# Dilated attention with rotary turning on 64 or on 128 partitions, a head's steps two or three blocks behind, and one sum of raw weights on POOL or on DVE

## The chip, the core and the metric

One core of a Trainium2 chip runs a block of two layers for 512 tokens of 1024 features in float32. The metric is the device time of one execution in microseconds (us), as the median of several. TensorE (PE) does the matmuls. VectorE (DVE), ScalarE (ACT) and GpSimd (POOL) work beside it, each through its own list of instructions in order, and SyncE (SP) starts the transfers of the weights. An engine that meets an instruction whose input isn't ready waits there, with all that stands behind it.

## The reference

Layer 0 mixes tokens by a gated recurrence, layer 1 by dilated attention; each is followed by a gated feed-forward part, and a vector `c` modulates norms and gates through `ada_w`. The change lies in layer 1:

```python
def apply_partial_rope(t, cos, sin):          # the first 32 of a head's 128 features
    t1, t2 = t[..., :16], t[..., 16:32]
    return concatenate([t1 * cos - t2 * sin, t2 * cos + t1 * sin, t[..., 32:]])

proj = (u @ w_in).reshape(B, S, 3, 3, 8, 128)       # group, q/k/v, head, feature
for gi, (window, dilation) in enumerate(((128, 1), (512, 4), (2048, 16))):
    q = apply_partial_rope(proj[:, :, gi, 0], cos, sin) * 128 ** -0.5
    k = apply_partial_rope(proj[:, :, gi, 1], cos, sin)
    o_g, lse_g = dilated_group_attention(q, k, proj[:, :, gi, 2], window, dilation)
wts = softmax(stack(lses))                          # weights of the three groups
o = einsum('gbsh,gbshd->bshd', wts, stack(outs))
y = o.reshape(B, S, 1024) @ w_out
```

## The kernel before

Each float32 product is made from three matmuls: weights and activations are cut into a high and a low part (`hi`, `lo`), and `three` (L427 to L430) multiplies hi by hi, lo by hi and hi by lo. ACT casts the high part of a weight tile (L84), and DVE subtracts it to get the low one (L85). `Stream` keeps two raw tiles of weights in flight and three pairs of parts. Its list `items` mixes attention weights with tiles of `ada_w`; these are reduced on DVE by one TENSOR_SCALAR (L245) and three SCALAR_TENSOR_TENSOR (L247) per tile, and then on POOL.

**Attention, 705 to 1126 us.** For each of 8 heads and 3 groups, two blocks of 24 matmuls of 128x512 make q and k, one block each. `qk_evac` (L1669) copies a block from the accumulator to `qk` (L1675) and its first 32 rows once more to a tile `turning` (L1676): q's rows on partitions 0 to 31, k's on 32 to 63, 512 tokens in columns. After k, `turn_pair` (L1680) turns both at once on DVE, by a shuffle of rows, two multiplications with the tables `cs` and an addition (L1683 to L1686), and ACT copies the results back into `qk` (L1689). For group 0 the copies and evacuations reorder the tokens, so they write strided.

A counter in `fl` (`Fillers`) ticks once per block. From the tick n at which a head starts, its steps are hung on later ticks: the scores of its three groups (L1710 for group 0, L1728 for groups 1 and 2) at n+2, n+4 and n+6, the merging weights at n+8, the transposes of the probabilities (`flips_r`, `flips_n`; matmuls L1777, their copies L1782 on ACT and L1784 on DVE) at n+9 and n+10, and the products with the values (`pv_r` L1804, `pv_n` L1813 and L1815) at n+10 and n+11. Steps of the last head, for which no blocks are left, go into `tail`, among the matmuls of the output projection.

**Values.** The values of groups 1 and 2 come from `seven_values`, which stands in the list of work after head 0's group 1 and again after head 4. A unit (one group, 512 features) takes two raw tiles of weights and makes four quarters of the product out of seven products of sums, each 24 matmuls of 128x256. `prepare` makes the operands: `cut` is a cast on ACT (L1371) and a subtraction on DVE (L1372). In its step 1, three sums on DVE (L1390 to L1392) follow a first sum on POOL (L1389); the casts of the later pieces use their results. The products are combined into V on DVE (L1426 to L1440).

The order of the instructions in each engine's list isn't the order of the code: a scheduler that estimates times orders them ahead of compilation. Time depends on which waits PE meets in that list.

Of the kernel before, what the change touches and what calls it, by code (L numbers as in the profile page):

```python
# [9 lines left out]
F32 = mybir.dt.float32  # L10
F32R = mybir.dt.float32r
I32 = mybir.dt.int32
AF = mybir.ActivationFunctionType
OP = mybir.AluOpType

P = 128
S = 512
# [18 lines left out]
class Stream:  # L36
# [31 lines left out]

    def fill(self):
        real = lambda i: self.items[i][1] is not None  # L70
        while self.loaded < len(self.items) and sum(map(real, range(self.done, self.loaded))) + real(self.loaded) <= self.raws:
            self._load(self.loaded)
            self.loaded += 1
# [78 lines left out]
def block_kernel(tc, x, c, positions, ada_w, ada_b, norm_g, hgrn_w_in, lower, hgrn_norm_g, hgrn_w_out,  # L152
# [8 lines left out]
    with ExitStack() as ctx:  # L161
# [38 lines left out]
        shared = base.tile([P, 4, S], F32, name="shared")  # L200
        cs = shared[:, 0:2]

# [209 lines left out]
        st = Stream(nc, wp, items, 2, 3)  # L412
# [300 lines left out]
        def rotary(pl):  # L713
# [10 lines left out]
            act.dma_start(invf, inv_freq)  # L724
            a0 = pl.tile([P, S], F32, name="a0")
            a1 = pl.tile([P, S], F32, name="a1")
            dve.tensor_copy(V4(a0), L4(pos_i))
            dve.tensor_scalar(a0, a0, invf, None, op0=OP.mult)
# [630 lines left out]
        def seven_values(dsts, apart, th, tl):  # L1359
# [17 lines left out]
            def prepare(i, step):  # L1377
                if i >= len(dsts):
                    return
                if step == 0:  # L1380
                    raws[i] = [st.whole(), st.whole()]
                    place(i, 0)
                    cut(i, 0, 0, 0, 0)
                    cut(i, 0, 1, 1, 1)
                elif step == 1:
                    place(i, 1)
                    cut(i, 1, 0, 1, 0)
                    a, b = raws[i]
                    pool.tensor_add(C(b, 1), C(b, 1), C(a, 1))  # L1389
                    dve.tensor_add(C(a, 1), C(a, 1), C(a, 0))  # L1390
                    dve.tensor_add(C(a, 0), C(a, 0), C(b, 1))
                    dve.tensor_add(C(b, 0), C(b, 0), C(a, 0))  # L1392
                    cut(i, 1, 1, 0, 0)
                elif step == 2:
                    place(i, 2)
                    cut(i, 2, 1, 0, 1)
                    cut(i, 2, 0, 1, 1)
                else:
                    place(i, 3)
                    cut(i, 3, 0, 1, 0)  # L1400
                    raws.pop(i)
                    st.fill()
# [235 lines left out]
        PNs, PR_h = [h[:, k].rearrange("p (t n) -> p t n", t=4) for k in range(2)], h[:, 2].rearrange("p (t n) -> p t n", t=4)  # L1638
        flip_no = [0]
        ap = cx.enter_context(tc.tile_pool(name="a_core", bufs=1))  # L1640
# [28 lines left out]
        def qk_evac(ps, g, k, pair):  # L1669

            tl = fresh(mk, [P, S], "qk", 6)
            scale = SCALE if k == 0 else 1.0
            if k == 0:
                pair.append(fresh(mk, [64, S], "turning", 1))
            act.activation(*((tl.rearrange("p (l r) -> p l r", r=4), R4(ps)) if g == 0 else (tl, ps)), AF.Copy, scale=scale)  # L1675
            act.activation(pair[0][k * 32:k * 32 + 32], ps[0:32], AF.Copy, scale=scale)  # L1676
            pair.append(tl)
            return tl

        def turn_pair(g, pair):  # L1680
            both = pair[0]
            rot = fresh(mk, [64, S], "rot", 1)
            dve.stream_shuffle(rot, both, [(i + 16) % 32 for i in range(32)])  # L1683
            dve.tensor_mul(rot, rot, cs[0:64, 1])
            dve.tensor_mul(both, both, cs[0:64, 0])
            dve.tensor_add(both, both, rot)  # L1686
            for k in range(2):
                dst, src = pair[1 + k][0:32], both[k * 32:k * 32 + 32]
                act.copy(*((dst.rearrange("p (l r) -> p l r", r=4), R4(src)) if g == 0 else (dst, src)))  # L1689

# [128 lines left out]
        for kind, g, i in order:  # L1819
            if kind == "v":  # L1820
                if g == 1:
                    seven_values(V[1:], apart, th, tl)
                    if i:
                        act.dma_start(V[0], v_away)
                continue
            if g == 0:
                heads[i] = {}
                n = fl.n
                fl.add(n + 2, lambda i=i: scores(i, 0))
                fl.add(n + 4, lambda i=i: scores(i, 1))  # L1830
                fl.add(n + 6, lambda i=i: scores(i, 2))
                fl.add(n + 8, lambda i=i: (merge_r(i), merge_n(i)))
                fl.add(n + 9, lambda i=i: flips_r(i))
                fl.add(n + 10, lambda i=i: pv_r(i))
                fl.add(n + 10, lambda i=i: flips_n(i))
                fl.add(n + 11, lambda i=i: pv_n(i))
            whi, wlo = st.take()
            pair = []
            for k in range(2):
# [6 lines left out]
        upx.close()  # L1846
        tail = {-1: [lambda: scores(7, 2), mkx.close], 2: [lambda: merge_r(7), back(0)], 3: [lambda: merge_n(7)],
                4: [lambda: flips_r(7)], 5: [lambda: pv_r(7), lambda: flips_n(7), back(2)], 6: [lambda: pv_n(7), back(1)],
# [34 lines left out]
```

## Time and profile before

| | us |
|---|---|
| Median of 3 runs (lowest, highest) | 1529.37 (1527.95, 1531.38) |
| The profiled execution's own time | 1529.39 |
| Its span, first to last instruction | 1527.7 |
| PE busy in it | 1502.0 |
| Stretch of the attention's blocks | 705 to 1126 |
| PE busy there, of 421.0 | 409.7 |
| DVE, ACT, POOL busy there | 292.5, 215.6, 53.1 |

Busy shares are averages over stages. Where an engine sat idle, the rows in order of time give in brackets the idle time just ahead of an instruction and what ended it. PE's clock can be granted at half for a time, and the rows of stretches show the mean of the granted clock, with 1.00 for the whole.

### The profile page before, as it was taken

The numbers are of one execution on the slowest core, as the hardware profiler recorded it, in microseconds if no ns is written. First come the engines' busy times: TensorE is split into PE (matmuls) and PEld (weight loads), VectorE is DVE, ScalarE is ACT, GpSimd is POOL, SyncE is SP. The second block draws the span as 40 slices with busy tenths as digits, with TensorE's granted clock in tenths as the row PEclk, the third lists the DMA queues.
The fourth block names the chain that finished last, engine by engine and source line by source line (L and its number), as shares of the span: only waits on it lengthen the run. The fifth ranks groups of instructions, "written<-read, shape, count | busy, mean of one in ns | idle before, by whom it ended". The sixth has DMA issues, their size and how long they took to land. (4 is left out here: it accounts for less than half of the span.)

```text
span 1527.7 us, 23466 instructions
## 1 busy us (share of the span) xinstructions
PE 1502.0 (98%) x9231; PEld 1318.2 (86%) x9231; DVE 1084.8 (71%) x1830; ACT 701.1 (46%) x1119; POOL 248.4 (16%) x212
## 2 busy tenths in 40 slices
PE   8999999999999999999998999999999999999998
PEld 6777888898999988888887888988888899999886
DVE  4587867486888896576667676677666978888633
ACT  4443433353444433384535554446555534444231
POOL 1012211131222212040101121111002222221100
PEclk9999999999999999999999999999999999999999
DMA  9554444125334356333166440265213333334531
GB/s 309 178 163 146 149 134 166 56 95 153 111 111 112 112 198 233 126 110 110 56 193 179 126 138 29 94 195 155 84 42 125 91 104 110 106 105 151 185 119 56
DMA packets 206942, 199.14 MB, mean 130 GB/s; under 512 B 6840, under 2 KB 164720, under 8 KB 206576
## 3 DMA queue, kind: packets, MB, share of 16 engines
q1 hardware_dynamic: 203856, 190.87, 40.6%
q10 hardware_dynamic: 1952, 6.65, 1.2%
q8 instruction: 72, 1.18, 0.3%
q0 software_dynamic: 1024, 0.13, 0.2%
q14 instruction: 38, 0.31, 0.1%
HBM read 192.31 MB, written 5.31 MB: 129 GB/s over the span
## 5 line engine op out<-in xcount | busy, mean ns | idle before, releaser
L85 DVE TENSOR_TENSOR lo<-raw,hi 128x2048 fp32r<-128x2048 f32 x68 | 163.5, 2406 | 90.7 <-ACT hi L84 90.5
L84 ACT CAST hi<-raw 128x2048 fp32r<-128x2048 f32 x68 | 129.9, 1910 | 195.1 <-DMA raw<-in_ffn_w_out_dram 55.8
L430 PE MATMUL ps_mm<-apart,lo 128*128 128x512 f32 x384 | 151.7, 395 | 0.0
L429 PE MATMUL ps_mm<-apart,hi 128*128 128x512 f32 x384 | 151.4, 394 | 0.0
L428 PE MATMUL ps_mm<-apart,hi 128*128 128x512 f32 x384 | 150.4, 392 | 0.0
L428 PE MATMUL ps_mm<-uh,hi 128*128 128x512 f32 (+1 forms) x400 | 146.3, 366 | 0.0
L429 PE MATMUL ps_mm<-ul,hi 128*128 128x512 f32 (+1 forms) x400 | 144.3, 361 | 1.0 <-DVE ul L528 1.0
L430 PE MATMUL ps_mm<-uh,lo 128*128 128x512 f32 (+1 forms) x400 | 144.5, 361 | 0.0
L808 ACT CAST hiq<-raw 128x1024 fp32r<-128x1024 f32 x68 | 68.3, 1050 | 65.5 <-DVE raw L796 64.5
L428 PE MATMUL ps_mm<-hi,oh 128*128 128x512 f32 x240 | 94.0, 392 | 0.0
L429 PE MATMUL ps_mm<-lo,oh 128*128 128x512 f32 x240 | 93.4, 389 | 0.0
L428 PEld LDWEIGHTS ps_mm<-uh,hi 128*128 128x128 f32 x400 | 75.5, 189 | 19.7 <-issue 8.4
L429 PEld LDWEIGHTS ps_mm<-ul,hi 128*128 128x128 f32 x400 | 75.6, 189 | 12.1 <-DVE ul L528 1.5
L430 PEld LDWEIGHTS ps_mm<-uh,lo 128*128 128x128 f32 x400 | 75.5, 189 | 11.4
L428 PEld LDWEIGHTS ps_mm<-apart,hi 128*128 128x128 f32 x384 | 72.4, 189 | 14.7
L430 PEld LDWEIGHTS ps_mm<-apart,lo 128*128 128x128 f32 x384 | 72.5, 189 | 14.3
L429 PEld LDWEIGHTS ps_mm<-apart,hi 128*128 128x128 f32 x384 | 72.3, 188 | 14.4
L247 DVE SCALAR_TENSOR_TENSOR shared<-raw,cond,shared 128x512 f32<-128x512 f32 x98 | 73.2, 747 | 11.5 <-DMA raw<-in_ada_w_dram 10.7
L812 DVE TENSOR_TENSOR loq<-raw,hiq 128x1024 fp32r<-128x1024 f32 x68 | 80.1, 1219 | 0.4 <-ACT hiq L808 0.4
L249 POOL PARTITION_ALL_REDUCE shared<-shared x14 | 48.4, 3459 | 183.3 <-DVE shared L247 176.4
L792 POOL TENSOR_TENSOR raw<-raw 128x512 f32<-128x512 f32 x34 | 54.6, 1605 | 104.2 <-DVE loq L788 47.7
L796 DVE TENSOR_TENSOR raw<-raw 128x1024 f32<-128x1024 f32 x34 | 41.7, 1225 | 39.1 <-POOL raw L792 39.1
(447 smaller groups left out, 4405.5 us busy)
## 6 DMA issues: line engine op xcount, KB each, us to landing
raw<-in_ada_w_dram SPq DMA_DIRECT2D x40, 1024.0 KB, 5.2
raw<-in_ffn_w_in_dram SPq DMA_DIRECT2D x136, 256.0 KB, 3.6
raw<-in_attn_w_in_dram SPq DMA_DIRECT2D x48, 512.0 KB, 5.2
raw<-in_ffn_w_out_dram SPq DMA_DIRECT2D x22, 1024.0 KB, 4.9
raw<-in_hgrn_w_in_dram SPq DMA_DIRECT2D x12, 1024.0 KB, 5.5
raw<-in_attn_w_in_dram SPq DMA_DIRECT2D x12, 1024.0 KB, 5.1
raw<-in_ffn_w_in_dram SPq DMA_DIRECT2D x10, 1024.0 KB, 5.1
first<-in_ada_w_dram SPq DMA_DIRECT2D x14, 512.0 KB, 7.6
```

What stands on the lines that cost most here:

```text
L84: self.nc.scalar.copy(hi, t)
L85: self.nc.vector.tensor_sub(lo, t, hi.bitcast(F32))
L247: dve.scalar_tensor_tensor(a, r[:, k], sc, a, op0=OP.mult, op1=OP.add)
L249: pool.partition_all_reduce(a, a, P, bass.bass_isa.ReduceOp.add)
L428: pe.matmul(ps, ah, bh, start=start, stop=False)
L429: pe.matmul(ps, ah, bl, start=False, stop=False)
L430: pe.matmul(ps, al, bh, start=False, stop=stop)
L792: pool.tensor_add(r[:, 2], r[:, 2], r[:, 0])
L796: dve.tensor_tensor(r[:, 0:2], r[:, 0:3:2], r[:, 1:2].broadcast_to((P, 2, 512)), op=OP.add)
L808: act.copy(hi, src)
L812: dve.tensor_sub(lo, src, hi.bitcast(F32))
```

## The change

It has four parts.

1. Turning works on 128 partitions and 256 columns: q's first half of tokens, q's second, k's first and k's second take 32 partitions each. Four ACT instructions of 256 columns fill them where two of 512 did, and stand ahead of the evacuation to `qk`. The four DVE operations have 256 columns instead of 512. Four copies of 256 columns bring the result back where there were two. The place is no longer a pool's tile with one buffer but two alternating slots in `shared`, which the smaller tables leave free. The tables are built by casts of four strips.
2. All steps of a head hang one tick later. Head 6's `pv_n` then falls behind the last block and goes into `tail`. What is due at the tick at which the values come is called ahead of them.
3. The first sum of a values' unit, L1389, moves from POOL to DVE.
4. `prepare` asks the stream for one more raw tile between the two cuts of its step 2.

Where the change moves instructions is decided by the scheduler. SP's list has the same transfers in the same order before and after, and POOL's is shorter by the four sums. In PE's list, head 0's first scores stand behind 20 matmuls of the first values' product before, and behind 10 after. The values' product `pv_n` of head 0 stands where all matmuls ahead of it take 2.95 us longer than before, at 227 ns for one of 512 columns, and the scores of head 1's group 2, next behind it, where they take 3.6 us longer.

DVE's list at the second values' unit; before, from the subtractions of its two raw tiles (6605 and 6684) on. L1372 is the subtraction of a `cut`, L1390 and L1391 are sums of raw tiles, the rows with V combine products:

```order
L1372 TENSOR_TENSOR loq_6742<-raw_6605,hiq_6741 128x1024
L1372 TENSOR_TENSOR loq_6742<-raw_6684,hiq_6741 128x1024
L1433 SCALAR_TENSOR_TENSOR V_6091<-V_6091,ps_mm_6772 128x2x256
L1372 TENSOR_TENSOR loq_6802<-raw_6684,hiq_6801 128x1024
L1434 TENSOR_TENSOR V_6091<-V_6091,ps_mm_6747 128x2x256
L1435 TENSOR_TENSOR V_6091<-V_6091,ps_mm_6747 128x2x256
L1440 TENSOR_TENSOR V_6091<-V_6091,ps_mm_6811 128x2x256
L1390 TENSOR_TENSOR raw_6605<-raw_6605 128x4x256
L1436 TENSOR_TENSOR V_6091<-V_6091,ps_a_6655 128x2x256
L1372 TENSOR_TENSOR loq_6838<-raw_6684,hiq_6837 128x1024
L1391 TENSOR_TENSOR raw_6605<-raw_6605,raw_6684 128x4x256
```

The same place after (raw tiles 6614 and 6636; lines are those of the changed kernel, where L1378 is the subtraction and L1395 to L1397 are the sums):

```order
L1378 TENSOR_TENSOR loq_6751<-raw_6636,hiq_6750 128x1024
L1440 SCALAR_TENSOR_TENSOR V_6094<-V_6094,ps_mm_6781 128x2x256
L1395 TENSOR_TENSOR raw_6636<-raw_6636,raw_6614 128x4x256
L1441 TENSOR_TENSOR V_6094<-V_6094,ps_mm_6756 128x2x256
L1442 TENSOR_TENSOR V_6094<-V_6094,ps_mm_6756 128x2x256
L1378 TENSOR_TENSOR loq_6811<-raw_6636,hiq_6810 128x1024
L1396 TENSOR_TENSOR raw_6614<-raw_6614 128x4x256
L1447 TENSOR_TENSOR V_6094<-V_6094,ps_mm_6820 128x2x256
L1443 TENSOR_TENSOR V_6094<-V_6094,ps_a_6666 128x2x256
L1378 TENSOR_TENSOR loq_6847<-raw_6636,hiq_6846 128x1024
L1397 TENSOR_TENSOR raw_6614<-raw_6614,raw_6636 128x4x256
```

The sum L1395 is new in DVE's list. From the subtraction of the second raw tile to the last sum shown stand ten operations before and eleven now.

ACT's list at head 1's group 0. Before, L84 is the cast of a weight tile, and L1689 copies the turned rows of q (7174) and k (7223):

```order
L1676 ACTIVATE turning_7175<-ps_mm_7149 32x512
L1675 ACTIVATE qk_7223<-ps_mm_7198 128x512
L1676 ACTIVATE turning_7175<-ps_mm_7198 32x512
L84 CAST hi_7240<-raw_7146 128x2048
L1689 COPY qk_7174<-turning_7175 32x512
L1689 COPY qk_7223<-turning_7175 32x512
L1675 ACTIVATE qk_7272<-ps_mm_7247 128x512
```

After (q is 7186, k is 7215, L87 is the cast of the same weight tile, raw 7158, L1702 the strided copy):

```order
L1686 ACTIVATE shared<-ps_mm_7190 32x256 x2
L1687 ACTIVATE qk_7215<-ps_mm_7190 128x512
L1702 COPY qk_7186<-shared 32x2x128 x2
L1702 COPY qk_7215<-shared 32x2x128 x2
L1754 ACTIVATE h,sR_7136<-h,nR_7137 128x256 x4
L87 CAST hi_7255<-raw_7158 128x2048
```

The copies went from behind the cast to ahead of it.

DVE's list at the turning of head 1's group 2, before. L245 and L247 reduce a tile of `ada_w`, and L1784 copies head 0's transposed probabilities for `pv_n`:

```order
L1683 STREAM_SHUFFLE rot_7469<-turning_7405 64x512
L245 TENSOR_SCALAR shared<-raw_7496,cond 128x512
L1784 COPY h<-ps_a_7418 128x384
L1684 TENSOR_TENSOR rot_7469<-rot_7469,shared 64x512
L1685 TENSOR_TENSOR turning_7405<-turning_7405,shared 64x512
L247 SCALAR_TENSOR_TENSOR shared<-raw_7496,cond,shared 128x512
L1686 TENSOR_TENSOR turning_7405<-turning_7405,rot_7469 64x512
L247 SCALAR_TENSOR_TENSOR shared<-raw_7496,cond,shared 128x512 x2
```

After:

```order
L1694 STREAM_SHUFFLE rot_7455<-shared 128x256
L1695 TENSOR_TENSOR rot_7455<-rot_7455,shared 128x256
L1696 TENSOR_TENSOR shared<-shared 128x256
L88 TENSOR_TENSOR lo_7511<-raw_7500,hi_7510 128x2048
L1697 TENSOR_TENSOR shared<-shared,rot_7455 128x256
L248 TENSOR_SCALAR shared<-raw_7508,cond 128x512
L250 SCALAR_TENSOR_TENSOR shared<-raw_7508,cond,shared 128x512 x3
L1799 COPY h<-ps_a_7474 128x384
```

The whole turning now stands ahead of the modulation, and the copy behind all four of its operations.

The diff, cut to what is named here:

```diff
-    def fill(self):
+    def fill(self, most=99):
         real = lambda i: self.items[i][1] is not None
         while self.loaded < len(self.items) and sum(map(real, range(self.done, self.loaded))) + real(self.loaded) <= self.raws:
+            if most == 0:
+                return
+            most -= 1
...
-        cs = shared[:, 0:2]
+        cs = shared[:, 0].rearrange("p (a n) -> p a n", a=2)
...
-            a0 = pl.tile([P, S], F32, name="a0")
-            a1 = pl.tile([P, S], F32, name="a1")
-            dve.tensor_copy(V4(a0), L4(pos_i))
+            a0 = pl.tile([P, 256], F32, name="a0")
+            a1 = pl.tile([P, 256], F32, name="a1")
+
+            for k in range(4):
+                j, r = slice(32 * k, 32 * k + 32), 2 * (k % 2)
+                dve.tensor_copy(a0[j].rearrange("p (r l) -> p r l", r=2), L4(pos_i)[j, r:r + 2])
...
-                    pool.tensor_add(C(b, 1), C(b, 1), C(a, 1))
+                    dve.tensor_add(C(b, 1), C(b, 1), C(a, 1))
...
                     cut(i, 2, 1, 0, 1)
+                    st.fill(1)
                     cut(i, 2, 0, 1, 1)
...
             if k == 0:
-                pair.append(fresh(mk, [64, S], "turning", 1))
+                flip_no[1] += 1
+                o = flip_no[1] % 2 * 256
+                pair.append(shared[:, 1, o:o + 256])
+            for hf in range(2):
+                o = k * 64 + hf * 32
+                act.activation(pair[0][o:o + 32], ps[0:32, hf * 256:hf * 256 + 256], AF.Copy, scale=scale)
             act.activation(*((tl.rearrange("p (l r) -> p l r", r=4), R4(ps)) if g == 0 else (tl, ps)), AF.Copy, scale=scale)
-            act.activation(pair[0][k * 32:k * 32 + 32], ps[0:32], AF.Copy, scale=scale)
...
-            rot = fresh(mk, [64, S], "rot", 1)
+            rot = fresh(mk, [P, 256], "rot", 1)
             dve.stream_shuffle(rot, both, [(i + 16) % 32 for i in range(32)])
-            dve.tensor_mul(rot, rot, cs[0:64, 1])
-            dve.tensor_mul(both, both, cs[0:64, 0])
+            dve.tensor_mul(rot, rot, cs[:, 1])
+            dve.tensor_mul(both, both, cs[:, 0])
             dve.tensor_add(both, both, rot)
             for k in range(2):
-                dst, src = pair[1 + k][0:32], both[k * 32:k * 32 + 32]
-                act.copy(*((dst.rearrange("p (l r) -> p l r", r=4), R4(src)) if g == 0 else (dst, src)))
+                for hf in range(2):
+                    dst, src = pair[1 + k][0:32], both[k * 64 + hf * 32:k * 64 + hf * 32 + 32]
+                    if g == 0:
+                        act.copy(L4(dst)[:, 2 * hf:2 * hf + 2], src.rearrange("p (r l) -> p r l", r=2))
+                    else:
+                        act.copy(dst[:, hf * 256:hf * 256 + 256], src)
...
                 if g == 1:
+
+                    for fn in fl.at.pop(fl.n, []):
+                        fn()
                     seven_values(V[1:], apart, th, tl)
...
-                fl.add(n + 2, lambda i=i: scores(i, 0))
-                fl.add(n + 4, lambda i=i: scores(i, 1))
-                fl.add(n + 6, lambda i=i: scores(i, 2))
-                fl.add(n + 8, lambda i=i: (merge_r(i), merge_n(i)))
-                fl.add(n + 9, lambda i=i: flips_r(i))
-                fl.add(n + 10, lambda i=i: pv_r(i))
-                fl.add(n + 10, lambda i=i: flips_n(i))
-                fl.add(n + 11, lambda i=i: pv_n(i))
+                fl.add(n + 3, lambda i=i: scores(i, 0))
+                fl.add(n + 5, lambda i=i: scores(i, 1))
+                fl.add(n + 7, lambda i=i: scores(i, 2))
+                fl.add(n + 9, lambda i=i: (merge_r(i), merge_n(i)))
+                fl.add(n + 10, lambda i=i: flips_r(i))
+                fl.add(n + 11, lambda i=i: pv_r(i))
+                fl.add(n + 11, lambda i=i: flips_n(i))
+                fl.add(n + 12, lambda i=i: pv_n(i))
...
-        tail = {-1: [lambda: scores(7, 2), mkx.close], 2: [lambda: merge_r(7), back(0)], 3: [lambda: merge_n(7)],
+        tail = {-1: [lambda: pv_n(6), lambda: scores(7, 2), mkx.close], 2: [lambda: merge_r(7), back(0)], 3: [lambda: merge_n(7)],
```

More of the change, by code (lines that the diff above doesn't have):

```diff
@@ L1638, in block_kernel @@
         PNs, PR_h = [h[:, k].rearrange("p (t n) -> p t n", t=4) for k in range(2)], h[:, 2].rearrange("p (t n) -> p t n", t=4)
-        flip_no = [0]
+        flip_no = [0, 0]
         ap = cx.enter_context(tc.tile_pool(name="a_core", bufs=1))
```

## The prediction

> **What bounds the kernel now.** I read the page's first part, then who TensorE waited for, then its instructions in order of time at each wait. The first part says that no faster engine elsewhere can help by itself:
>
> ```profile
> span 1527.7 us, 23466 instructions
> PE 1502.0 (98%) x9231; PEld 1318.2 (86%) x9231; DVE 1084.8 (71%) x1830; ACT 701.1 (46%) x1119; POOL 248.4 (16%) x212
> ```
>
> TensorE (PE) is idle for 1527.7 - 1502.0 = 25.7 us in the whole program. The change keeps every matmul, so it can win only in waits of PE, and in matmuls that run slowly. Nearly all that it touches lies in the attention stage, 705 to 1126 us. There the long waits are these (start, duration, engine, line, operation; in brackets the idle time before it and who ended it):
>
> ```profile
> 731.36 1.79 PE L1710 MATMUL ps_a<-qk,qk 128*128 128x128 f32 x8 [1.55 <-ACT qk L1689]
> 762.51 0.50 PE L428 MATMUL ps_mm<-hiq,uh 128*128 128x256 f32 x2 [2.09 <-ACT hiq L1371]
> 811.68 1.57 PE L1710 MATMUL ps_a<-qk,qk 128*128 128x128 f32 x7 [1.87 <-ACT qk L1689]
> 838.39 0.49 PE L1815 MATMUL ps_b<-h,V 128*128 128x128 f32 x2 [1.32 <-DVE h L1784]
> 842.20 2.02 PE L1728 MATMUL ps_a<-qk,qk 128*128 128x128 f32 x8 [2.42 <-ACT qk L1689]
> ```
>
> and, in the view of waits of the same stretch, the short ones (in all, times, longest):
>
> ```profile
> PE ps_b L1813 <- ACT h L1782: 0.7, 1, 0.7
> PE ps_a L1777 <- DVE sN L1715: 0.5, 1, 0.5
> PE ps_a L1777 <- DVE h L1772: 0.5, 1, 0.5
> PE ps_b L1804 <- ACT h L1782: 0.4, 1, 0.4
> ```
>
> The five long ones are 9.25 us, the short ones 2.1. To them comes the clock. The view of stretches, 5 us behind three of the waits (span of the stretch, then busy time of PE, PEld, DVE, ACT, POOL; then the granted clock):
>
> ```profile
> 762.50:767.50 5.00, 4.99 (x29) 4.99 (x30) 4.27 (x12) 1.04 (x1) 0.00 (x0) 0.66 0.29 80
> 811.70:816.70 5.00, 5.00 (x23) 4.26 (x24) 2.02 (x12) 4.99 (x13) 0.78 (x2) 1.00 0.53 142
> 842.20:847.20 5.00, 5.00 (x19) 4.36 (x20) 3.06 (x23) 2.14 (x8) 0.00 (x0) 0.66 0.77 208
> ```
>
> Behind the waits of 2.09 and 2.42 us the granted clock was 0.66 over 5 us: each lost (1 - 0.66) x 5 = 1.7 us more. Behind 1.87 it stayed 1.00. So in this program a wait that passes about 2 us costs its length and 1.7 us. **All that can be won** in this stage is 9.25 + 2.1 + 3.4 = 14.75 us, 1.0%.
>
> [...]
>
> **The change, part by part.** What its edits cost, from groups of the same stage (count | busy, mean ns):
>
> ```profile
> L1676 ACT ACTIVATE turning<-ps_mm 32x512 f32<-32x512 f32 x48 | 28.1, 584 | 0.6
> L1689 ACT COPY qk<-turning 32x512 f32<-32x512 f32 x46 | 36.3, 789 | 24.8 <-DVE turning L1686 18.2 <-DVE wZ L1754 3.5 <-DVE wZ L1756 2.6
> L1720 ACT ACTIVATE h<-h,nN 128x256 f32<-128x256 f32 x24 | 11.8, 494 | 0.0
> L1720 ACT ACTIVATE h<-h,nN 128x128 f32<-128x128 f32 x8 | 3.2, 401 | 15.6 <-DVE nN L1717 15.6
> ...
> L1683 DVE STREAM_SHUFFLE rot<-turning 64x512 f32<-64x512 f32 x24 | 17.4, 727 | 0.0
> L1684 DVE TENSOR_TENSOR rot<-rot,shared 64x512 f32<-64x512 f32 x24 | 16.3, 679 | 0.1
> L1715 DVE CUSTOM_DVE_ANT_0 h<-ps_a,maskN 128x256 f32<-128x256 f32 x24 | 9.3, 417 | 0.0
> ```
>
> *Turning by halves.* ACT's half pieces (256 columns) are in no row. They cost at least half of 584, 292 ns, and at most 584. The two exponential rows give 93 ns for each 128 columns, so 256 columns fewer would take 584 - 186 = 398: I take 0.40, and 0.43 to 0.65 for the strided copies of group 0. A pair then needs 4 x 0.40 + 4 x 0.40 = 3.2 us of ACT instead of 2 x 0.584 + 2 x 0.789 = 2.75, for group 0 up to 4.2. For 24 pairs that is 11 to 25 us more on an engine that is 46% busy. DVE's three arithmetic operations fall from 0.68 to about 0.41 (between 0.34, the half, and the 0.417 of the last row), the shuffle from 0.73 to about 0.45 (between 0.36 and 0.73). A pair has 2.77 before and 1.68 after: 1.1 us less, 26 us in all. None of this is on PE, so it counts only through the waits. The smaller rotary tables and the four casts for them stand far ahead of this stage, where no PE wait hangs on them: nothing, either way at most a microsecond.
>
> *Raw sums on DVE.* Four sums leave POOL and become DVE work of the size of L1390. The first unit's chain in before, ahead of the wait at 731.36 (POOL, DVE, DVE, ACT):
>
> ```profile
> 718.63 3.31 POOL L1389 TENSOR_TENSOR raw<-raw,raw 128x1024 f32<-128x1024 f32 x1 [41.19 <-DVE loq L1372]
> ...
> 721.98 1.23 DVE L1390 TENSOR_TENSOR raw<-raw 128x1024 f32<-128x1024 f32 x1 [2.29 <-POOL raw L1389]
> ...
> 728.36 0.68 DVE L1686 TENSOR_TENSOR turning<-turning,rot 64x512 f32<-64x512 f32 x1
> ...
> 729.13 2.18 ACT L1689 COPY qk<-turning 32x512 f32<-32x512 f32 x2 [2.58 <-DVE turning L1686]
> ```
>
> After: from 718.47 to 721.98 DVE now does its own sum (1.2, ends 719.6) and L1390 (ends 720.8) instead of waiting, 2.3 us ahead; the rotation's shorter pieces add up to about the last 0 to 0.3. With the order shown, the last addition ends near 727.0 instead of 729.0, and the four strided copies (1.7 to 2.6) end at 728.7 to 729.6, against 731.3. But the scores now stand 10 matmuls earlier in PE's order (10 x 0.12 = 1.2), so PE comes at 729.81 - 1.2 = 728.6. A wait of 0.1 to 1.0 stays of the 1.55: **-0.5 to -1.4, I take -0.9.**
>
> The second unit, ahead of the wait at 762.51 (DVE, then ACT):
>
> ```profile
> 742.18 1.23 DVE L1372 TENSOR_TENSOR loq<-raw,hiq 128x1024 fp32r<-128x1024 f32 x1 [3.62 <-ACT hiq L1371]
> ...
> 750.74 1.23 DVE L1372 TENSOR_TENSOR loq<-raw,hiq 128x1024 fp32r<-128x1024 f32 x1 [4.87 <-ACT hiq L1371]
> ...
> 752.48 3.11 DVE L1372 TENSOR_TENSOR loq<-raw,hiq 128x1024 fp32r<-128x1024 f32 x1
> ...
> 757.30 1.21 DVE L1390 TENSOR_TENSOR raw<-raw 128x1024 f32<-128x1024 f32 x1
> ...
> 760.17 1.21 DVE L1391 TENSOR_TENSOR raw<-raw,raw 128x1024 f32<-128x1024 f32 x1
> ...
> 749.66 2.00 ACT L1371 CAST hiq<-raw 128x1024 fp32r<-128x1024 f32 x2 [6.33 <-DMA raw<-in_attn_w_in_dram]
> 761.41 1.04 ACT L1371 CAST hiq<-raw 128x1024 fp32r<-128x1024 f32 x1 [1.81 <-DVE raw L1391]
> ```
>
> The subtraction at 752.48 took 3.11 instead of 1.23 while POOL summed beside it: 1.9 us lost. From 750.74 to the end of L1391 (761.3, when ACT's cast of its result could start) are 10.6 us. After, by the rows of the order: three subtractions (1.14 from start to start), the new sum, L1390 and L1391 (1.13 each) and five operations on V (0.6 each), 9.8 us. And the chain starts sooner: the second raw tile is loaded into the one that the subtraction at 742.18 frees, which stands behind the first head's softmax and its copies on ACT; the scores ahead of these start 1.2 + 0.9 = 2.1 sooner, a shuffle and two multiplications ahead of the softmax's sums give 0.8, and ACT's copies take 0.4 longer. Of these 2.5 I take 1.9 to 2.3, since ACT's evacuations lie in between. Together 2.7 to 3.1 us sooner, against the 2.09 of the wait and the 0.9 that PE itself comes sooner: 0 to 0.3 us of wait, and no half clock. **-2.0 - 1.7 = -3.7.** Had only the contention gone, the wait would be 2.09 + 0.9 - 1.9 = 1.1 and the clock still whole.
>
> *One block later, and the order.* At 811.68 PE waited for two copies behind a cast that waited for a weight transfer:
>
> ```profile
> 807.59 1.91 ACT L84 CAST hi<-raw 128x2048 fp32r<-128x2048 f32 x1 [6.35 <-DMA raw<-in_attn_w_in_dram]
> 809.40 2.22 ACT L1689 COPY qk<-turning 32x512 f32<-32x512 f32 x2
> ```
>
> In the new order of ACT these copies stand ahead of that cast, so they don't wait for its 6.35 us. **-1.9.**
>
> The waits at 838.39 and 842.20 have one cause (DVE, DVE, DVE, ACT, and the issue with its time to landing):
>
> ```profile
> 837.38 0.49 DVE L245 TENSOR_SCALAR shared<-raw,cond 128x512 f32<-128x512 f32 x1 [2.76 <-DMA raw<-in_ada_w_dram]
> 837.79 0.55 DVE L1784 COPY h<-ps_a 128x384 f32<-128x384 f32 x1
> ...
> 840.12 0.68 DVE L1686 TENSOR_TENSOR turning<-turning,rot 64x512 f32<-64x512 f32 x1
> ...
> 840.88 1.26 ACT L1689 COPY qk<-turning 32x512 f32<-32x512 f32 x2 [6.09 <-DVE turning L1686]
> ...
> raw<-in_ada_w_dram SPq DMA_DIRECT2D x1, 1024.0 KB, 8.6
> ```
>
> A modulation transfer landed late (8.6 us), and behind the DVE instruction that waited for it stood the copy for the values' product and the rest of head 1's last rotation. In the new order the whole rotation stands ahead of that instruction, so the second wait goes, with its clock: -2.4 - 1.7. The copy, though, now stands behind that instruction and three more of its kind (0.49 + 3 x 0.75 = 2.7 us). The values' product comes 2.95 us later in PE's order than before, and so this is about even if the transfer lands in its usual time: -1.3, with a remainder that I count below. **-5.4.**
>
> *Freed sooner.* The added fill changes no row of SP's order, and the next raw tile's load was already issued when its last reader ended. Nothing.
>
> *What is late next.* The four short waits are of kinds that the change leaves (a flip's copy, a softmax's sum): I let them stand. New order, new short waits: for the copies that are now eight ACT instructions a pair, for the copy behind the modulation, and for the weights behind the second unit's chain (which only DVE now carries). I allow five of the size of those seen (0.5): **+2.5.**
>
> Sum: -0.9 - 3.7 - 1.9 - 5.4 + 2.5 = -9.4. The profiled execution took 1529.39 us, 1.7 more than its span and as good as the median of the runs, 1529.37: **1520.0 us.**
>
> **The rivals.**
>
> *Half of it only.* Two of the terms hang on transfers. If the modulation transfer lands late again, the copy behind four DVE instructions waits 1.3 + 2.3 = 3.6 us and takes the 1.7 of clock with it: the -5.4 becomes -0.1, and the time is 1525.3. If besides this the second unit's chain is not 2.7 us sooner but only as much as the contention (1.9), its term falls to -1.0 - 1.7 = -2.7 and the time is 1526.3. For it speaks the row of 8.6 us; against it, that one transfer of the stage did so.
>
> *The change doesn't do what it says.* "One block later" moves the steps in the code; but PE's order puts head 0's first scores 1.2 us earlier than before. Copies that end as late as now would then be waited for longer: the 731.36 wait becomes 1.55 + 1.2 = 2.75 and takes the clock, +2.9 instead of -0.9, and the one at 811.68 stays. With the other terms: -9.4 + 3.8 + 1.9 = -3.7, 1525.7, or within 0.2% if a third term goes too.
>
> *Slower.* The mechanism is ACT's queue ahead of scores. Copies and evacuations become eight instructions of 0.4 to 0.65, 0.5 to 1.5 us more for a pair, and scores wait for the last. As three of five long waits already are for L1689, 1 us more at a pair with no slack makes a wait of about 2 us, and from 2.09 on it costs 3.8 with the clock. One such wait in a head takes 8 x 3.8 = 30 us, 1541 with the other gains kept; it is slower from four such waits on (4 x 3.8 = 15.2, against 9.4: 1535). Against it: 21 of the 24 pairs had no wait for their copies, and the DVE part in front of these is 1.1 us shorter, about what ACT adds.
>
> **How the numbers follow.** The forecast, 1520.0, has 0.70 with its surroundings from 1515 to 1525; half of it or the order at fault 0.20 (1524 to 1529); slower 0.10. The low end is all that can be won, 1529.4 - 14.7 = 1514.7. The high end is 1529.5, where the half cases end. About 0.2% (3 us) is what a measurement of this kernel can tell from no change: of the half cases 0.07 are still faster than 1526.3 and 0.13 are within; of the slower mechanism 0.02 are within, with three waits of 3.8 against the 9.4. Faster 0.77, within 0.15, slower 0.08.
>
> **What would show it.** In the new profile, PE should wait under 1 us at the first scores, not at all for a cast of the second unit, and for no copy behind a cast that waits for a transfer; the granted clock should read 1.00 through 705 to 1126. POOL loses four sums (10.5 us), DVE has four more of 1.2 us and 24 pairs near 1.7. Wrong would be: a wait of over 2 us for the rotation's copies in more than one head, a subtraction at 3 us without POOL beside it, half pieces on ACT near 0.58, or a copy of the p0 flip that PE waits for in several heads.

## The result and the profile after

The changed kernel takes 1520.96 us (median of 4 runs, 1520.42 to 1521.52), against 1529.24 for the kernel before, measured beside it (4 runs); the ratio is 0.9945, 95% interval 0.9927 to 0.9962. The forecast was 1520.0. The profiled execution took 1520.42 us, and its page begins:

```profile
span 1518.7 us, 23536 instructions
...
PE 1501.0 (99%) x9231; PEld 1316.2 (87%) x9231; DVE 1061.3 (70%) x1837; ACT 719.0 (47%) x1215; POOL 235.2 (15%) x208
```

DVE does 23.5 us less (1084.8 - 1061.3), ACT 17.9 more, POOL 13.2 less, and PE does what it did. The view of PE's waits from 700 to 1120 us has these and no others (in all, times, longest):

```profile
PE ps_b L1819 <- ACT h L1797: 1.5, 2, 1.1
PE ps_a L1725 <- ACT qk L1702: 1.1, 1, 1.1
PE ps_a L1792 <- DVE h L1780: 0.7, 1, 0.7
PE ps_b L1828 <- ACT h L1797: 0.5, 1, 0.5
PE ps_b L1818 <- DVE h L1799: 0.3, 1, 0.3
PE ps_a L1743 <- DVE h L1799: 0.2, 1, 0.2
```

That is 4.3 us in place of 11.35, none is above 1.2, and the clock stays whole (1.00 over 705 to 1117 us). Its view of stretches has the second values' unit without a gap (7.00 us busy in 7.00), and 1.00 for the clock there and over 727 to 767 us:

```profile
727.00:767.00 40.00, 38.91 (x317) 38.36 (x316) 24.76 (x45) 20.15 (x32) 1.65 (x2) 1.00 0.27 78
757.00:764.00 7.00, 7.00 (x62) 7.00 (x61) 7.00 (x14) 2.11 (x2) 0.00 (x0) 1.00 0.03 8
```

To compare stretches of kernels whose clocks start a little apart, I take the start of the matmul of the same number (each kernel has 9231) in two traces and see how much further ahead the other kernel is from one mark to the next. Ahead of each mark stands the same work in every kernel, except at 4950, where up to five matmuls of 128 columns have changed places with five of 512. At 0.13 and 0.227 us each that moves, as an estimate, up to 0.5 us between the two rows that meet there. Before minus after:

| from matmul to matmul | what lies there in the trace of before | gained, us |
|---|---|---|
| 0 to 4200 | everything ahead of attention, 1 to 682 us | -0.7 |
| 4200 to 4500 | the first scores, 731 us | 0.5 |
| 4500 to 4800 | the second values' unit, 762 us | 3.65 |
| 4800 to 4950 | head 1's copies, 811 us | 1.6 |
| 4950 to 5100 | flips, values' products and last scores of heads 0 and 1, 829 to 842 us | 3.35 |
| 5100 to 6900 | the rest of attention | 0.6 |
| 6900 to 9230 | everything after, from 1180 us | 0.0 |

The first row is scatter of the start: in the twelve profiles of the experiments below it lies between a gain of 1.0 and a loss of 2.2, and no edit touches that part except the tables. Part of it is the clock: over the first 25 us its mean is 0.93 in before and 0.86 in after (a loss of 0.7). Over the whole profile it is 0.999 in e1 and e4 (gains of 1.0 and 0.5), 0.996 in e3 and 0.995 in e8 (losses of 2.2 and 2.0), where one later half clock each is counted in.

### The profile page after: what moved, and what is told of

It is laid out like the page before. It is cut to its first block, busy times and chain, and to the rows that moved or that the text cites. A ratio compares the mean times of both kernels' runs of the same rounds, so it can differ in the third digit from the quotient of the medians.

```text
span 1518.7 us, 23536 instructions
## 1 busy us (share of the span) xinstructions
PE 1501.0 (99%) x9231; PEld 1316.2 (87%) x9231; DVE 1061.3 (70%) x1837; ACT 719.0 (47%) x1215; POOL 235.2 (15%) x208
## 5 line engine op out<-in xcount | busy, mean ns | idle before, releaser
L88 DVE TENSOR_TENSOR lo<-raw,hi 128x2048 fp32r<-128x2048 f32 x68 | 158.8, 2336 | 94.3 <-ACT hi L87 94.1
L87 ACT CAST hi<-raw 128x2048 fp32r<-128x2048 f32 x68 | 129.8, 1908 | 193.6 <-DMA raw<-in_ffn_w_out_dram 55.6
```

The source lines that it names most:

```text
L87: self.nc.scalar.copy(hi, t)
L88: self.nc.vector.tensor_sub(lo, t, hi.bitcast(F32))
```

## The experiments

The first theory was that of the prediction: each part clears its own wait. Its main rival was that the parts can stand in for each other, since a wait goes as soon as whatever ends last comes early enough. In the table the gains are those of the table above, read in one profile each, with its last two rows as "rest"; "ratio" is against the kernel before, with 11 to 28 runs of it measured beside each group.

| run | median, us | ratio, 95% interval | first scores | second unit | head 1's copies | 829 to 842 | rest |
|---|---|---|---|---|---|---|---|
| e1 no halves | 1520.54 | 0.9945, 0.9925 to 0.9964 | 0.3 | 1.75 | 1.2 | 4.5 | 0.0 |
| e2 not later | 1522.62 | 0.9961, 0.9947 to 0.9976 | 0.4 | 3.8 | 1.4 | 1.1 | 1.8 |
| e3 sum on POOL | 1521.68 | 0.9949, 0.9928 to 0.9970 | 0.6 | 3.8 | 1.6 | 3.3 | 0.5 |
| e4 sum alone | 1520.16 | 0.9941, 0.9922 to 0.9960 | 0.2 | 2.3 | 2.1 | 3.5 | 0.7 |
| e5 halves alone | 1522.03 | 0.9962, 0.9949 to 0.9976 | 0.55 | 3.6 | 1.6 | 4.9 | -3.2 |
| e6 later alone | 1523.98 | 0.9976, 0.9964 to 0.9989 | 0.05 | -0.04 | 1.0 | 5.9 | -2.7 |
| e7 swap | 1526.80 | 0.9989, 0.9977 to 1.0000 | 0.04 | -0.3 | 1.8 | -0.2 | 0.0 |
| e8 no fill | 1521.10 | 0.9953, 0.9938 to 0.9968 | 0.5 | 3.7 | 1.6 | 1.85 | 0.2 |
| e9 hook | 1522.55 | 0.9950, 0.9937 to 0.9963 | 1.7 | -1.5 | 1.6 | 3.95 | 0.1 |
| e10 modulation later | 1519.62 | 0.9934, 0.9921 to 0.9947 | 0.4 | 3.6 | 2.0 | 7.1 | -3.5 |
| e11 both | 1523.33 | 0.9962, 0.9948 to 0.9975 | 1.7 | -0.2 | 2.0 | 7.1 | -4.0 |
| e12 the change again | 1519.80 | 0.9935, 0.9921 to 0.9950 | 0.5 | 3.5 | 1.6 | 4.5 | 0.7 |

Runs of one kernel lie several us apart (the kernel before took 1523.7 to 1532.3 in 28 runs), so a difference of 2 us between two of these kernels isn't settled by their medians. What a single wait does is read in the profiles.

**e1: the change without its first part**

```diff
-                pair.append(shared[:, 1, o:o + 256])
+                pair.append(fresh(mk, [64, S], "turning", 1))
-            rot = fresh(mk, [P, 256], "rot", 1)
+            rot = fresh(mk, [64, S], "rot", 1)
```

with the two evacuations, two copies and wide tables of before.

> The changed kernel with the turning of before (64 partitions, 512 columns, two copies); sums on DVE and steps one block later stay. Theory (each part clears its own waits, the halves those at head 1's copies and at the modulation): the second unit's cast stays clear, the copies of head 1's group 0 stand behind the cast that waits for a transfer again and PE waits 1.5 to 2 us there, and the turning of head 1's group 2 stands behind the modulation again; time 1524 to 1527. Rival (one block later cleared those waits): no wait over 1 us at head 1, 1520 to 1522.

The theory's time was wrong and the rival's was right: 1520.54. The theory's waits were there in part: head 1's copies stand behind the cast again, but PE waits 0.6 us and not 1.5 to 2 for them. For these copies that is the rival's "no wait over 1 us at head 1"; among head 1's blocks a transpose of head 0 does wait 1.62 us, for DVE's scaling of the probabilities. Without the halves PE waits 1.28 us at the first scores and 1.05 at the second unit, and neither costs clock: the mean of the granted clock over the whole profile is 0.999.

**e2: the change without its second part**

```diff
-                fl.add(n + 3, lambda i=i: scores(i, 0))
+                fl.add(n + 2, lambda i=i: scores(i, 0))
```

and so on for the other seven, with `pv_n(6)` out of `tail` and the added call ahead of the values gone.

> The changed kernel with a head's steps at n+2 to n+11 as before; halves and sums on DVE stay. Theory (one block later only gives the values' product of head 0 its 3 us): that product waits 1 to 4 us for the copy behind the modulation, and the rest stays clear; 1521 to 1525. Rival (one block later is what cleared head 1's scores): waits of 1.9 and 2.4 us for head 1's copies come back, the second with a half clock; 1526 to 1528.

The time is inside the theory's range, but by another wait than the theory's: head 0's values' product, for which it had 1 to 4 us, doesn't wait. Group 2's own wait of 842 us doesn't come back, but a new one stands nearby, longer than any in the kernel before, with the half clock behind it (0.50 over 831 to 834 us). PE's row, then ACT's and DVE's ahead of it, and POOL's all-reduce of the modulation:

```profile
830.96 1.41 PE L1743 MATMUL ps_a<-qk,qk 128*128 128x128 f32 x5 [3.76 <-ACT qk L1704]
...
827.41 1.90 ACT L87 CAST hi<-raw 128x2048 fp32r<-128x2048 f32 x1 [4.83 <-DMA raw<-in_attn_w_in_dram]
830.44 1.67 ACT L1704 COPY qk<-shared 32x256 f32<-32x256 f32 x4 [0.15 <-DVE shared L1697]
...
827.42 2.47 DVE L1696 TENSOR_TENSOR shared<-shared 128x256 f32<-128x256 f32 x1
830.26 0.55 DVE L1799 COPY h<-ps_a 128x384 f32<-128x384 f32 x1
...
827.28 3.32 POOL L252 PARTITION_ALL_REDUCE shared<-shared  x1 [6.62 <-DVE shared L250]
```

These are the scores of head 1's group 1, whose own copies had ended some 10 us before; the copies that the view names belong to group 2. What ended last for them is very likely DVE's copy of a flip out of the accumulator (L1799, ended at 830.81): in the change's own profile the same scores wait 0.19 us, put down to that copy. Ahead of it on DVE stands a multiplication of the turning that takes 0.42 elsewhere and took 2.47 here, beside POOL's all-reduce. The change has such a multiplication too (826.76, in the last section), but its steps stand one block later, and PE comes to these scores at 835.4 and not at 827.2. In e5, whose steps stand where e2's do, the same scores wait 2.13 for that copy. So one block later gives room for what is late on DVE there; with the halves and the sum in place it isn't needed against the particular wait of 842 us that the prediction spoke of.

**e3: the change without its third part**

```diff
-                    dve.tensor_add(C(b, 1), C(b, 1), C(a, 1))
+                    pool.tensor_add(C(b, 1), C(b, 1), C(a, 1))
```

> The changed kernel with the first raw sum on POOL again; halves and later steps stay. Theory (the sum cleared the second unit): PE waits about 2 us for the second unit's cast with the half clock behind it, and a subtraction on DVE takes about 3.1 us beside the sum; 1524 to 1525.5. Rival (the shorter turning on DVE cleared it): wait under 1 us there and clock 1.00, 1520.5 to 1522.

The rival was right about the wait and the time: the second unit gains 3.8 us with its sum on POOL. Its reason, the shorter turning, is only a part, though. The rows, POOL first, then DVE:

```profile
751.44 2.40 POOL L1395 TENSOR_TENSOR raw<-raw,raw 128x1024 f32<-128x1024 f32 x1 [6.93 <-DVE loq L1378]
...
751.93 0.69 DVE L1441 TENSOR_TENSOR V<-V,ps_mm 128x512 f32<-128x512 f32 x1
752.54 0.68 DVE L1442 TENSOR_TENSOR V<-V,ps_mm 128x512 f32<-128x512 f32 x1
753.14 1.79 DVE L1378 TENSOR_TENSOR loq<-raw,hiq 128x1024 fp32r<-128x1024 f32 x1
```

Two operations on V, which read the accumulator, now stand beside POOL's sum, and they take their usual 0.68. The subtraction, which reads the tiles `raw` and `hiq`, comes late, 0.7 us ahead of the sum's end at 753.84, and took 1.79, against 1.23 alone. In the kernel before it came first and took 3.11, 1.9 more than alone. The new order gave the chain what the move to DVE was to give it.

**e4: the kernel before with the sum alone**

```diff
-                    pool.tensor_add(C(b, 1), C(b, 1), C(a, 1))
+                    dve.tensor_add(C(b, 1), C(b, 1), C(a, 1))
```

> The kernel before with only the first raw sum moved to DVE. Theory: the waits at the first scores (1.55) and at the second unit (2.09, with 1.7 of half clock) shrink, together 4 to 5 us, the rest stays; 1524 to 1526. Rival (1.2 us more on DVE for each unit takes the place of POOL's): a wait of over 1.5 us stays at the second unit; 1527.5 to 1530.

It was faster than either expected, 1520.16: one line gives all that the change gives, as far as the intervals tell. At the second unit half the wait stays,

```profile
760.96 0.50 PE L428 MATMUL ps_mm<-hiq,uh 128*128 128x256 f32 x2 [1.05 <-ACT hiq L1371]
```

and no half clock follows (the mean over the whole profile is 0.999), so 2.3 of the 3.7 us are gained. The waits at 811 and 842 us are gone as well, though no edit touched what they wait for. Relative to PE the weights came earlier: the modulation tile that landed at 837.36 in before, 2.4 us ahead of PE's arrival at the last scores of head 1 (842.20 - 2.42 = 839.78), landed at 830.88 here, 8.5 us ahead of its arrival at 839.37. Of these 6.1 us, 1.6 are a shorter transfer (7.0 instead of 8.6), and 4.1 are PE's order: the last scores of head 1 begin with matmul 5044 in before and with 5062 here, 18 matmuls of 512 columns at 0.227 us later. The edit touches neither; the scheduler moved them.

**e5 to e7: one part alone, and a control**

e5 adds only the first part to the kernel before (the lines of e1 the other way round), e6 only the second. e7 adds no work and takes none away:

```diff
-            act.activation(*((tl.rearrange("p (l r) -> p l r", r=4), R4(ps)) if g == 0 else (tl, ps)), AF.Copy, scale=scale)
             act.activation(pair[0][k * 32:k * 32 + 32], ps[0:32], AF.Copy, scale=scale)
+            act.activation(*((tl.rearrange("p (l r) -> p l r", r=4), R4(ps)) if g == 0 else (tl, ps)), AF.Copy, scale=scale)
```

> The kernel before with the turning by halves alone. After e3 and e4 the theory is that two parts are each enough by themselves: here the scheduler puts two operations on V beside POOL's sum, so no subtraction is held for 1.9 us, the second unit's wait is under 1 us with no half clock, and head 1's copies stand ahead of the cast; 1520 to 1522.5. Rival (the sum has to leave POOL): 2 us and the half clock at the second unit; 1524 to 1526.

> The kernel before with all steps one block later, sums on POOL, turning on 64 partitions. Theory: DVE's order at the second unit is that of before, so the subtraction stands beside POOL's sum at 3.1 us, the wait of about 2 us and its half clock stay, and so do head 1's copies behind the cast; 1525 to 1529. Rival (any other order of the steps removes the waits): 1519 to 1522.

> The kernel before with only the two evacuations of a block swapped (rows for the turning first, then the whole), no work added or removed. A control. Theory: the second unit's order is that of before and its wait of 2 us and half clock stay; 1526 to 1530. Rival (before is an unlucky order, and any other is 8 us faster): 1519 to 1522.

At the second unit all three came out as the theory had it. e5 has no wait there. In e6, where DVE's order is that of before (POOL, DVE, PE),

```profile
751.21 2.40 POOL L1389 TENSOR_TENSOR raw<-raw,raw 128x1024 f32<-128x1024 f32 x1 [7.56 <-DVE loq L1372]
...
751.58 3.11 DVE L1372 TENSOR_TENSOR loq<-raw,hiq 128x1024 fp32r<-128x1024 f32 x1
...
761.62 0.79 PE L428 MATMUL ps_mm<-hiq,uh 128*128 128x256 f32 x2 [2.11 <-ACT hiq L1371]
```

the subtraction takes 3.11 again and the wait is 2.11 with the half clock (the two matmuls behind it take 0.79 us, and 0.50 in e4); e7 has 3.11 and 2.19. This is the chain of the prediction, shown in three kernels (before, e6, e7). Where the whole subtraction doesn't stand beside a sum on POOL (e1, e3, e4, e5, the change), the wait is 1.05 us (e1, e4) or none, and the clock stays whole: it reads 1.00 there in the change and 0.999 over the whole of e1 and e4, and e3 and e5 gain as much there (3.8 and 3.6 us) as the change. The control gains nearly 2 us at head 1's copies and nothing elsewhere, and keeps 842's wait (2.43) with its half clock (matmuls of 512 columns 0.43 us apart from 842.56 to 844.70, and 0.23 from 845.12 on): another order of the evacuations alone does not give what the change gives. e6 was faster than its range: with later steps alone that last wait went.

At 829 to 842 us e5 and e6 gain more than the change, and they lose it later: "rest" is -3.2 and -2.7. Each has one new long wait with the half clock behind it (0.66 over 1041.2 to 1046.2 us in e5; in e6 four matmuls take 1.22 us, and 0.61 without a wait in e8), e5 then e6:

```profile
1041.16 1.16 PE L1824 MATMUL ps_b<-h,V 128*128 128x128 f32 x4 [2.19 <-ACT h L1793]
...
1045.39 1.22 PE L1813 MATMUL ps_b<-h,V 128*128 128x128 f32 x4 [2.60 <-ACT h L1782]
```

It is a values' product that waits for a copy of transposed probabilities, which stands on ACT behind a cast that had itself waited 4.04 us (e5) and 5.98 us (e6) for a weight transfer. In the change the cast waits 3.20 us there, and PE 0.5. So one such wait costs each of these two, in its profile, over 3 us against the change.

**e8: the change without its added fill**

```diff
-                    st.fill(1)
```

> The changed kernel without the added fill in step 2. Theory: the lists of PE, DVE, ACT and SP are those of the change but for names, so 1519.5 to 1522, as with it. Rival (the earlier fill frees the raw tile sooner): 2 us or more over it.

1521.10, as the change. Its lists have the same instructions in the same order, so its profile and that of e12 show how much one kernel differs between executions: at 829 to 842 us it gained 1.85, the change 3.35 and 4.5.

**e9 to e12: can it be bettered?**

e9 calls head 0's first scores behind the first product of the values (a function passed to `seven_values`), e10 lets the modulation tiles of heads 0 to 4 begin later in the stream and follow each other more closely, and e11 does both. e12 is the change itself.

```diff
-                    seven_values(V[1:], apart, th, tl)
+                    seven_values(V[1:], apart, th, tl, due[0] if due else None)
...
-        woven(late[:8], 1.5)
+        woven(late[:8], 0.8, 6)
```

(`woven` passes the second number on as the distance and the third as the first place in the list.)

> The changed kernel with head 0's first scores called behind the first product of the values instead of ahead of it; in PE's list they move back by 104 matmuls of 256 columns. Theory: the wait of 1.1 us for their strided copies goes, and the second unit's chain has the slack for the later softmax; 1 us less than the change, 1518.5 to 1521. Rival (the softmax now stands between the second unit's operands): a wait of 1 us or more at the second unit; as the change or slower, 1521 to 1525.

> The changed kernel with the eight modulation tiles of heads 0 to 4 woven in from the seventh weight tile on (heads 2 to 4), not from the first. Theory (the waits at head 0's and head 1's flips and scores, 815 to 845 us, come from weight transfers that share the queue with modulation tiles, and from copies behind their DVE work): PE waits there fall under 0.7 us in all; 1518 to 1520.5. Rival (the waits go where the modulation goes): waits of 2 us or more in heads 3 and 4, 1521 to 1524.

> Both edits of e9 and e10 on the changed kernel. Theory: they add up, 3 us less than the change, 1516.5 to 1519. Rival: either rival of e9 or e10 holds; 1520 or more.

> The changed kernel itself once more, beside e9 to e11 on the same chip: 1520 to 1522.5 by the runs so far.

e9 went as its rival said. In PE's list the first scores moved back by 14 matmuls (from 4409 to 4423) and not by the 104 expected. The wait of 1.1 us went and two new ones came, PE's view:

```profile
759.50 1.16 PE L1745 MATMUL ps_a<-qk,qk 128*128 128x128 f32 x8 [1.65 <-DVE V L1445]
761.71 0.67 PE L431 MATMUL ps_mm<-hiq,uh 128*128 128x256 f32 x2 [1.05 <-ACT hiq L1377]
```

with the half clock behind them (0.50 over 762 to 764 us): 5.2 us less at the second unit than in the change (-1.5 against 3.65), for 1.2 more at the first scores. e10 shows both theories at work. The stretch at 829 to 842 us gains 7.1 us instead of 3.35 to 4.5 and has no wait left, which fits waits that come from the modulation in the stream; then head 3 pays where the modulation now stands,

```profile
892.75 1.71 PE L1725 MATMUL ps_a<-qk,qk 128*128 128x128 f32 x7 [2.51 <-ACT qk L1702]
```

and the rest loses 3.5. Its time, 1519.62, can't be told from e12's 1519.80, which itself lies just under the 1520 to 1522.5 expected of it. e11 has the losses of both (-0.2 at the second unit, -4.0 in the rest) and came out as its rival said, 1523.33: the two edits don't add up. None of the versions is shown to beat the change.

## Why the prediction was right, and where it wasn't

- **Size and sum.** The attention stage gained 9.7 us in the profiles (0.5 + 3.65 + 1.6 + 3.35 + 0.6), against a forecast of 9.4. What PE could win was bounded well by its idle time and clock. That the sum fits to 0.3 us is luck in part: over the same stretches e12, the same kernel, gained 10.9, and e8, with the same lists, 7.8.
- **First scores.** Forecast 0.9, got 0.5: PE still waits 1.09, just over the 1 us named as the limit. The last addition ended at 727.7 and not 727.0, but PE too was 0.7 us late by then in this trace (the first row of the table), so this cancels. What is left is the strided copies: they took 0.64 each, the upper end of what was allowed, and end at 730.4:

```profile
727.26 0.42 DVE L1697 TENSOR_TENSOR shared<-shared,rot 128x256 f32<-128x256 f32 x1
...
727.77 2.60 ACT L1702 COPY qk<-shared 32x256 f32<-32x256 f32 x4 [1.35 <-DVE shared L1697]
```

- **Half pieces.** Forecast 0.40 for evacuations and plain copies, 0.41 for DVE's arithmetic, 0.45 for the shuffle; measured 0.37 and 0.40, 0.42, 0.44. The groups of the profile after:

```profile
L1686 ACT ACTIVATE shared<-ps_mm 32x256 f32<-32x256 f32 x96 | 35.9, 374 | 16.8 <-PE ps_mm L433 15.7
L1704 ACT COPY qk<-shared 32x256 f32<-32x256 f32 x62 | 25.0, 403 | 13.6 <-DVE shared L1697 12.5 <-DVE wZ L1771 0.3
L1702 ACT COPY qk<-shared 32x256 f32<-32x256 f32 x32 | 20.6, 643 | 6.0 <-DVE sR L1751 4.3 <-DVE shared L1697 1.3
...
L1694 DVE STREAM_SHUFFLE rot<-shared 128x256 f32<-128x256 f32 x24 | 10.7, 444 | 0.0
L1697 DVE TENSOR_TENSOR shared<-shared,rot 128x256 f32<-128x256 f32 x24 | 10.0, 417 | 0.1
```

- **Second unit.** Forecast 3.7, got 3.65. The chain took 9.9 us, where 9.8 were worked out, from 749.16 to the end of the sum that the cast waits for:

```profile
749.16 1.23 DVE L1378 TENSOR_TENSOR loq<-raw,hiq 128x1024 fp32r<-128x1024 f32 x1 [4.07 <-ACT hiq L1377]
...
757.84 1.22 DVE L1397 TENSOR_TENSOR raw<-raw,raw 128x1024 f32<-128x1024 f32 x1
```

  By the trace's time it began 1.6 us sooner; against PE, which was 0.7 late in this trace, 2.3, the upper end of the 1.9 to 2.3 allowed. What didn't hold is the heading: "Raw sums on DVE" isn't needed for this gain. e3 has it without, by the order that the halves brought; e4 has 2.3 us of it with the sum alone.
- **Head 1's copies.** Forecast 1.9, got 1.6. The copies went ahead of the cast as the rows said: they start at 801.33, and PE's scores come at 805.82 without a wait. (Up to 0.5 us of this gain is counted in the next row, as said above.) But this stood under "One block later, and the order", and e6 shows that one block later leaves them behind the cast (0.90 us of wait): the first part moved them, and e5 has no wait there. Nor is the move needed: in e4 and in the control the copies still stand behind a cast that waits 2.42 and 5.84 us for its transfer, and PE doesn't wait. Its scores come 9 and 3 matmuls later in its list than before.
- **Waits at 838 and 842.** Forecast 5.4 less about 2.5 of new waits, together 2.9; got 3.35 and 0.6. The late transfer of before wasn't a single event, as the argument against the first rival ("one transfer of the stage did so") supposed. The longest of the four transfers issued from 814 to 829 us took 10.3 us in e7, 9.0 in e2, 7.0 in e4 and 6.6 in the change's profile. The wait of 842 us went in every one of these kernels but the control, with the sum alone too, so no single part can be named as its cure. PE's list goes with it in part: the scores that waited begin with matmul 5044 in before and 5046 in the control, where the wait stays, and with 5051 to 5067 where it is gone, except in e2, where they begin with 5037, behind the wait of 3.76. No run moved them alone, so how much the order does and how much the transfers stays open. So does why transfers slow there in some executions: no run took the load of the stretch apart.
- **The parts don't add up.** Alone, the sum, the halves and the later steps gain 0.59%, 0.38% and 0.24%; together 0.55% to 0.65%. Taking any one out of the change leaves 0.39% to 0.55%. The prediction added terms site by site, which gave the right total, and gave each site to one part, which was wrong. At the second unit the halves alone clear the whole wait (e5), the sum alone clears the half clock and half of the wait (e4), and later steps alone nothing (e6). That several parts can do the same work was none of its rivals.
- **The slower rival** didn't come: one pair's copies are waited for, for 1.1 us. Its 1541 takes the other gains off twice; by its own terms, 1529.4 + 30 - 9.4, it is 1550.

## What to carry to other kernels

When one engine is busy 98% of the time, list its waits and the clock behind them: that is the whole budget, and here a forecast that went wait by wait came close to the sum. To learn which edit cleared a wait, undo each edit alone and make each alone: a wait goes when the last of several chains comes early enough, so several edits can each be sufficient, and a one-line one may do. A control that only reorders (e7) tells a cured cause from a lucky order.

## What the runs showed of the hardware

**Half clock behind waits of about 2 us, though not behind each.** In before the granted clock is 0.50 for 3.41 us from 16.26, from 763.78 and from 842.28 us, 747.52 and 78.51 us apart (219 and 23 times 3.413); the last two drops follow the waits of 2.09 and 2.42 us. A wait of 1.99 us in e8 brought the half clock, one of 2.13 in e5 didn't (PE's rows and the stretches behind them, e8 then e5):

```profile
821.80 1.00 PE L1792 MATMUL ps_a<-ident,h 128*128 128x128 f32 x3 [1.99 <-DVE h L1780]
821.80:826.80 5.00, 5.00 (x18) 4.04 (x19) 4.05 (x14) 3.89 (x9) 0.77 (x1) 0.66 1.14 313
...
833.28 0.94 PE L1739 MATMUL ps_a<-qk,qk 128*128 128x128 f32 x6 [2.13 <-DVE h L1795]
833.30:838.30 5.00, 5.00 (x37) 4.74 (x38) 4.83 (x23) 0.00 (x0) 0.17 (x1) 1.00 0.80 210
```

Over 5 us the clock is 0.66 behind the first and 1.00 behind the second. In e9 neither wait reaches 2 us: they are 1.65 and 1.05, and the clock behind them is 0.97 over 760 to 762 us, 0.50 over 762 to 764 and 0.68 over 764 to 766. By these means the half clock began at 761.88, and in the 3.41 us ahead of that (from 758.47 on) lie 1.03 of the first wait and 1.05 of the second, together as much as one wait of 2.08. In e3 a wait of 2.09 was followed by 0.51 over 829.2 to 832.6 us. So the prediction's limit, a wait that passes about 2 us, is an estimate from three waits of before: e5 passes it without the half clock, and e9 has the half clock without one such wait. How idle time counts was not shown.

**Some DVE instructions took longer beside POOL's.** A subtraction of two tiles took 3.11 us beside POOL's sum (before, e6, e7) and 1.23 alone. In these three and in e3, where it took 1.79, it ended 1.08 to 1.09 us after the sum did. Operations with one input from the accumulator kept their 0.68 (e3). The turning's multiplications took longer beside PARTITION_ALL_REDUCE: besides the 2.47 us of e2, in the changed kernel's profile one of 0.42 took 2.70:

```profile
826.76 2.70 DVE L1695 TENSOR_TENSOR rot<-rot,shared 128x256 f32<-128x256 f32 x1
...
827.00 3.18 POOL L252 PARTITION_ALL_REDUCE shared<-shared  x1
```

It took 2.28 us more than its usual 0.42, and ended at 829.46, 0.7 us before the all-reduce did (830.18). In e2 the multiplication ended 0.7 us before the all-reduce too. So the subtraction ended about its own time behind POOL's sum, and the multiplication ahead of the all-reduce's end; why they differ was not shown.
